# Two feed-forward openings reordered, one weight sum of each made by DMA, and 18 products ahead of the first load

## The chip, the core and the metric

The kernel runs on one core of a Trainium2 chip. Five engines work side by side, each on its own queue of instructions in a fixed order: TensorE (PE in the profile, with its weight loads as PEld), VectorE (DVE), ScalarE (ACT), GpSimd (POOL) and SyncE (SP). SP issues most DMAs, POOL a few of its own. An instruction starts when the one ahead of it on its queue has let it through and all that it waits for is done. The metric is the device time of one execution, in microseconds.

## The reference

One step of a decoder trunk on 520 tokens (512 of a prompt and 8 single samples), in float32:

```python
h = h + 0.5 * _swiglu(_rms_norm(h, ffn1_norm), w1_gate, w1_up, w1_down)
m, ... = _hybrid_mixer(_rms_norm(h, mix_norm), states, weights)   # pooling heads and a state-space scan
h = h + m
h = h + 0.5 * _swiglu(_rms_norm(h, ffn2_norm), w2_gate, w2_up, w2_down)
return _rms_norm(h, final_norm), new states

def _swiglu(x, wg, wu, wd):
    return (silu(x @ wg) * (x @ wu)) @ wd          # 1024 -> 2816 -> 1024
def _rms_norm(x, g):
    return x * rsqrt(mean(x * x) + 1e-6) * g
```

The change touches the first few microseconds of the two feed-forward parts, FFN1 and FFN2. Both compute the same thing from different weights.

## The kernel before

Activations stand transposed: 8 tiles of 128 features (D = 1024) by 520 tokens, the tokens in two halves of 260 (HB). A float32 product is made of three products in a faster format (`mm3`: L117, L120, L121): the weights are split into a high part `whi` (a cast on ACT, L107) and a low part `wlo` (a subtract on DVE, L108), the activations into `xth` and `xtl`.

Gate and up projection are a two-by-two block product over features and token halves, done by 7 products in place of 8 (class `Ffn`), as in Strassen's scheme. That needs sums of activations and sums of weights.

- For every block f of 128 columns of the 2816 (22 blocks) SP loads `raw` (two DMAs of 512 KB; `load`, L255 and L256). `raw` has two buffers. `whi`/`wlo` `a` is the split of its first half, `b` of a quarter of it. Weight sums: s1 is one DVE operation of 128x1024 (L262), s2 two of 128x512 (L263, L264), both split again into shi/slo `c` (of s1) and `d` (of s2).
- The seven products are numbered as in `product`; A (one PSUM bank) takes products 1, 6, 7 and 4, BE (two banks) takes 2, 5 and 3. A and BE have two buffers. After products 1, 6, 7 and 5 ACT copies the bank to `ac` (L299) before the next product goes on in it.
- The activations: `scaled` makes xg (x times the norm's gain, ACT, L181), `prep_pair` makes four differences xd of xg (DVE, L188 to L192) and splits xg and xd into `xth` (ACT, L195) and `xtl` (DVE, L196), for four pairs j = 0..3 of feature tiles.
- The norm's 1/rms isn't applied ahead of the products but behind them: `squares` sums the squares (ACT L157, DVE L158), `rstd` sums over partitions by a product with a tile of ones (psr, L163), takes the root on ACT (L164, which needs its own activation table; `ACT_TABLE_LOAD` in the trace) and the reciprocal on DVE (L165), for each token half. The result r_f is multiplied in behind the product.

**The openings.** While xg, its splits and r_f are being made, PE has nothing for the seven products. So the first blocks are done "plain": in float32 proper, without splits or sums (`plain`, L234; four P banks of each block; one such product leaves two records in the trace). FFN1 does f = 0 and f = 1 in this way (`direct` = 2), FFN2 only f = 0. `plain_out` finishes such a block: two multiplies by r_f on DVE (tg, L241), Silu on ACT (L243, again with a table load), two multiplies by the up half on DVE (L245), and the split of the result g (L247, L248). The first block by seven products is f = 2 in FFN1, and f = 1 in FFN2, whose weights are prepared under the mixer.

The order of the instructions of each engine isn't written out: a scheduler at build time places them by modelled times, with `tc.high_priority()` for parts that shall go early, and `tc.issue_after(ins)`, which lets nothing of the enclosed code that runs on the engine of `ins` be placed ahead of it. `behind[2]` holds the instruction behind which f = 2's load is placed: the second of `plain_out(0)`'s multiplies by r_f, in both FFNs. SP's loads wait for free buffers: f = 2's `raw` for the last product that reads f = 0's, f = 3's for the last readers of f = 2's first buffer, among them L264.

POOL does little here. It issues the loads of the states (br, hs) for the state output, which is worked into FFN2's stream.

Of the kernel before, what the change touches and what calls it, by code (L numbers as in the profile page):

```python
# [62 lines left out]
def tile_trunk_step(ctx: ExitStack, tc: tile.TileContext, ins: dict, outs: dict):  # L63
# [96 lines left out]
    def rstd(r, acc, hs, width, name):  # L160
        ps = bank(f"psr_{name}")[:, : hs.stop - hs.start]
        for k, sq in enumerate(acc):
            nc.tensor.matmul(ps, ones, sq, start=k == 0, stop=k == len(acc) - 1)  # L163
        nc.scalar.activation(out=r[:, hs], in_=ps, func=AF.Sqrt, bias=eps, scale=1.0 / width)  # L164
        nc.vector.reciprocal(out=r[:, hs], in_=r[:, hs])  # L165

    def rstds(nx, name):
        for b, hs in enumerate(HALVES):
            rstd(nx[3], [nx[2][:, hs]], hs, D, f"{name}{b}")
# [15 lines left out]
    def prep_pair(nx, gp, nb, xg, j, name):  # L185
        xth, xtl, _, _ = nx
        xd = gp.tile([P, 4, HB], F32, tag="g", bufs=nb, name=f"xd_{name}{j}")
        nc.vector.tensor_tensor(out=xd[:, 0:2], in0=xg[:, 0::2], in1=xg[:, 3:4].to_broadcast([P, 2, HB]),  # L188
                                op=ALU.subtract)
        nc.vector.scalar_tensor_tensor(out=xd[:, 2], in0=xd[:, 1], scalar=-1.0, in1=xg[:, 0], op0=ALU.mult,  # L190
                                       op1=ALU.subtract)
        nc.vector.scalar_tensor_tensor(out=xd[:, 3], in0=xd[:, 2], scalar=-1.0, in1=xg[:, 1], op0=ALU.mult,  # L192
                                       op1=ALU.subtract)
        for s, t in ((xg[:, 0:3], slice(0, 3)), (xd, slice(3, 7))):
            nc.scalar.copy(xth[:, j, t], s)  # L195
            nc.vector.tensor_tensor(out=xtl[:, j, t], in0=s, in1=xth[:, j, t].bitcast(F32), op=ALU.subtract)  # L196

    class Ffn:
# [52 lines left out]
        def load(self, f):  # L251
# [5 lines left out]
            d1 = split(raw[:, 0], 1024, f"{n}a", wp, 3, ("whi", "wlo"))  # L257
# [4 lines left out]
            nc.vector.tensor_tensor(out=s1, in0=diag, in1=up0, op=ALU.add)  # L262
# [14 lines left out]
        def product(self, f, p):  # L277
            js = range(KD // 2)
            if f not in self.A:
                with tc.issue_after(self.behind[f]) if f in self.behind else nullcontext():  # L280
                    self.load(f)
                n = f"{self.i}_{f}"
                self.A[f] = ps[0].tile([P, 512], F32, tag="A", bufs=2, name=f"A{n}")
                self.BE[f] = ps[0].tile([P, 2, 512], F32, tag="BE", bufs=2, name=f"BE{n}")
                self.ac[f] = [self.wx.tile([P, 2, HB], F32, tag="ac", bufs=3, name=f"ac{n}_{q}") for q in range(2)]
# [12 lines left out]
            if keep is not None:  # L298
                nc.scalar.copy(keep, out[:, :HB])  # L299
# [17 lines left out]
        def scales(self):  # L317
            rstds(self.nx, f"f{self.i}")
# [129 lines left out]
    xg1 = []  # L448
    for j in range(KD // 2):
# [9 lines left out]
        prep_pair(nx1, g1, NG, xg1[j], j, "f1")  # L459
    ffn1.plain_load(1)  # L460
    with tc.high_priority():
        ffn1.scales()
# [3 lines left out]
    with tc.high_priority():  # L466
        ffn1.behind[2] = ffn1.plain_out(0)
# [36 lines left out]
    def fill(j):  # L504
        if not j:
            f2["ffn"].plain_load(0)
        f2["ffn"].plain(0, f2[j], j)
        prep_pair(f2["ffn"].nx, f2["xg"], 4, f2[j], j, "f2")
# [613 lines left out]
```

## Time and profile before

| | |
|---|---|
| median of 3 runs | 993.05 us (991.81 to 993.05) |
| profiled execution | 992.8 us, span 991.0 us |
| granted TensorE clock (mean) | 0.997 |
| TensorE (PE) busy | 969.8 us, 98% |
| VectorE (DVE) busy | 800.0 us, 81% |
| ScalarE (ACT) busy | 552.8 us, 56% |
| GpSimd (POOL) busy | 87.4 us, 9% |
| HBM traffic | 114 GB/s over the span |
| FFN1's opening | from 0 to about 41 us |
| FFN2's opening | from about 637 to 655 us |

In a row of the timeline stand the start (us from the span's start), the duration, the engine, the line of the kernel, the operation, its output and inputs by the program's names, the shape and how many equal ones follow; in square brackets the idle time of that engine just before, and what ended it. A row of the waits names the waiting instruction, its releaser, and the total, the number and the longest of the waits in us. Busy times of PE are modelled ends of pipelined products, so a PE that is busy is not necessarily at its peak. The profiled execution's time is 1.8 us longer than its span.

### The profile page before, as it was taken

How to read it: one execution, taken by the hardware profiler on the slowest of the kernel's cores; microseconds unless marked ns; L12 is line 12 of the kernel's file. 1: busy time of each engine (PE TensorE's matmuls, PEld its weight loads, DVE VectorE, ACT ScalarE, POOL GpSimd, SP SyncE). 2: the span in 40 equal slices, each digit the busy share in tenths (PEclk: the TensorE clock that was granted, in tenths of full speed). 3: DMA queues.
4: the chain of work that ended last, by engine and by line, in shares of the span. 5: the costliest groups of instructions: out<-in, count | busy, mean ns of one | idle time of the engine just before them, and what ended most of it. 6: DMA issues, size and time to landing. Idle time of an engine off the chain costs nothing.

```text
span 991.0 us, 19414 instructions
## 1 busy us (share of the span) xinstructions
PE 969.8 (98%) x7852; PEld 951.0 (96%) x7852; DVE 800.0 (81%) x1295; ACT 552.8 (56%) x1011; POOL 87.4 (9%) x157
## 2 busy tenths in 40 slices
PE   7999999999999999999999999999999999999996
PEld 6899999999999999999899999899999999999995
DVE  7999656997569688788978997999967899668876
ACT  7566414664136455685668574666643566534653
POOL 0000000000000000156522000100013000120000
PEclk9999999999999999999999999999999999999998
DMA  6332322323222232262335232323246423363212
GB/s 188 121 128 95 120 86 86 128 86 129 85 86 81 91 126 85 82 206 100 124 114 186 81 125 86 113 98 128 100 117 198 162 88 127 120 181 119 96 65 87
DMA packets 42027, 114.48 MB, mean 116 GB/s; under 512 B 6408, under 2 KB 13512, under 8 KB 41936
## 3 DMA queue, kind: packets, MB, share of 16 engines
q1 hardware_dynamic: 38864, 103.78, 30.6%
q0 software_dynamic: 3072, 9.44, 3.7%
q8 instruction: 62, 1.02, 0.4%
q14 instruction: 29, 0.24, 0.1%
HBM read 105.86 MB, written 7.34 MB: 114 GB/s over the span
## 4 chain that ended last, share of the span: by engine, by line
PE 90%; DVE 5%; POOL 1%; DMA 1%; issue 1%; ACT 1%; SPq 0%; DVEq 0%; ACTq 0%
PE A L121 8%; PE A L117 8%; PE A L120 8%; PE dn L121 7%; PE dn L117 7%; PE dn L120 7%; PE BE L117 6%; PE BE L121 6%; PE BE L120 6%; PE wo L117 2%; PE wo L121 2%; PE wo L120 2%; PE P L234 2%; PE inz L117 2%; PE inz L121 2%; PE inz L120 2%
## 5 line engine op out<-in xcount | busy, mean ns | idle before, releaser
L117 PE MATMUL dn<-g,whi_1d 128*128 128x260 f32 x352 | 99.3, 283 | 0.2 <-DVE td L369 0.2
L120 PE MATMUL dn<-g,whi_1d 128*128 128x260 f32 x352 | 99.5, 283 | 0.0
L121 PE MATMUL dn<-g,wlo_1d 128*128 128x260 f32 x352 | 99.4, 283 | 0.0
L369 DVE SCALAR_TENSOR_TENSOR td<-dn,r_f 128x520 f32<-128x520 f32 x40 | 27.8, 698 | 72.7 <-PE dn L121 72.7
L121 PE MATMUL dn<-g,wlo_2d 128*128 128x260 f32 x256 | 72.5, 283 | 0.8 <-DVE wlo_2d L108 0.8
L117 PE MATMUL dn<-g,whi_2d 128*128 128x260 f32 x256 | 72.3, 282 | 0.0
L120 PE MATMUL dn<-g,whi_2d 128*128 128x260 f32 x256 | 72.3, 282 | 0.0
L117 PEld LDWEIGHTS dn<-g,whi_1d 128*128 128x128 f32 x352 | 66.1, 188 | 0.4 <-DVE td L369 0.4
L120 PEld LDWEIGHTS dn<-g,whi_1d 128*128 128x128 f32 x352 | 66.3, 188 | 0.0
L121 PEld LDWEIGHTS dn<-g,wlo_1d 128*128 128x128 f32 x352 | 66.2, 188 | 0.0
L299 ACT COPY ac<-A 128x260 f32<-128x260 f32 x123 | 45.6, 374 | 28.9 <-PE A L121 28.0
L107 ACT CAST whi_1d<-raw_1d 128x1024 fp32r<-128x1024 f32 (+1 forms) x24 | 23.5, 981 | 67.0 <-PE dn L120 54.2
L262 DVE TENSOR_TENSOR s<-raw 128x1024 f32<-128x1024 f32 x41 | 49.9, 1218 | 5.6 <-DMA raw<-in_w2gu 5.6
L234 PE MATMUL P<-xg_f,raw 128*128 128x260 f32 x192 | 45.4, 392 | 6.4 <-ACT sq_f L157 5.5
L121 PEld LDWEIGHTS dn<-g,wlo_2d 128*128 128x128 f32 x256 | 48.2, 188 | 1.0 <-DVE wlo_2d L108 1.0
L234 PEld LDWEIGHTS P<-xg_f,raw 128*128 128x128 f32 x192 | 36.9, 196 | 12.2 <-ACT sq_f L157 5.4
L117 PEld LDWEIGHTS dn<-g,whi_2d 128*128 128x128 f32 x256 | 48.3, 189 | 0.0
L120 PEld LDWEIGHTS dn<-g,whi_2d 128*128 128x128 f32 x256 | 48.2, 188 | 0.0
L117 PE MATMUL wo<-catg,whi_wo 128*128 128x260 f32 x128 | 37.2, 290 | 0.0
L117 PE MATMUL inz<-xh_mx,whi_inz 128*128 128x260 f32 x128 | 36.8, 287 | 0.1
L117 PE MATMUL inx<-xh_mx,whi_inx 128*128 128x260 f32 x128 | 36.4, 284 | 0.0
L121 PE MATMUL wo<-catg,wlo_wo 128*128 128x260 f32 x128 | 36.2, 283 | 0.0
(1341 smaller groups left out, 3936.7 us busy)
## 6 DMA issues: line engine op xcount, KB each, us to landing
raw<-in_w2gu SPq DMA_DIRECT2D x44, 512.0 KB, 4.5
raw<-in_w1gu SPq DMA_DIRECT2D x42, 512.0 KB, 4.5
raw_1d<-in_w1d SPq DMA_DIRECT2D x16, 512.0 KB, 4.5
raw_2d<-in_w2d SPq DMA_DIRECT2D x16, 512.0 KB, 4.4
raw_wo<-in_w_out SPq DMA_DIRECT2D x12, 512.0 KB, 4.9
ab<-scr_acs SPq DMA_DIRECT2D x8, 512.0 KB, 4.9
h<-in_state_ssm SPq DMA_DIRECT2D x16, 256.0 KB, 3.7
raw_inz<-in_w_in SPq DMA_DIRECT2D x8, 512.0 KB, 3.8
```

What stands on the lines that cost most here:

```text
L107: nc.scalar.copy(h, src)
L117: first = nc.tensor.matmul(ps, whi, xhi, start=start, stop=False, **kw)
L120: nc.tensor.matmul(ps, whi, xlo, start=False, stop=False, **kw)
L121: nc.tensor.matmul(ps, wlo, xhi, start=False, stop=stop, **kw)
L234: nc.tensor.matmul(self.banks[f, u][b][:, :HB], ws(self.raw[f][:, u], j + 4 * q), xg[:, slot[q]], start=j == q == 0, stop=j == 3 and q == ...
L262: nc.vector.tensor_tensor(out=s1, in0=diag, in1=up0, op=ALU.add)
L299: nc.scalar.copy(keep, out[:, :HB])
L369: nc.vector.scalar_tensor_tensor(out=t, in0=banks[d][:, :, :HB], scalar=-0.5, in1=self.nx[3].rearrange("p (b t) -> p b t", b=2), op0=ALU.mult,
```

## The change

1. 18 products of the 128x128 tile `ones` with itself are put at the head of PE's queue; nobody reads their bank.
2. FFN1: the split of the last pair's xd (j = 3; one ACT cast, one DVE subtract) is taken out of `prep_pair` and made later: the cast behind the second root on ACT, the subtract behind `plain_out(0)`'s second multiply by r_f (`free`) on DVE.
3. `mark`, a GpSimd copy of one column of the last xg, is placed on POOL. The DMAs of point 4 are placed behind it in FFN1.
4. For f = 2 of both FFNs s1 isn't summed on DVE. POOL issues three DMAs instead: two copy quarters of the weights from HBM into s1 (256 KB each), the third adds another quarter to both halves of s1 (512 KB, an accumulating DMA).
5. `behind` now has three parts: the split `a` is placed behind the first, the sums behind the second, and the third says whether s1 is made by DMA. FFN1: `(free,)`, then `(free, root, mark)`. FFN2: the last xd operation, then `plain_out(0)`'s `free`.
6. FFN2: product 1 of f = 1 is issued ahead of `scales`, and `scales` (psr, root, reciprocal) is placed behind that product's copy `ac` on ACT (`kept`) and behind the last `xtl` on DVE (`low`).

As the scheduler places it, only the two openings change their order: about the first 255 instructions of PE, and some 185 of them around FFN2's opening. SP's order stays as it is. On ACT, FFN1's shi_2c now stands ahead of whi_2a, whi_2b and Silu; in FFN2 shi_2c stands behind the cast of g. On PE, FFN2's product 1 of f = 2 now comes right behind product 1 of f = 1, and products 6, 7 and 4 of f = 1 follow each other.

```diff
@@ -88,6 +88,12 @@
     eps = cst.tile([P, 1], F32, tag="eps", name="eps")
     nc.vector.memset(eps, EPS)
 
+    def queued(*ins):
+        stack = ExitStack()
+        for i in ins:
+            stack.enter_context(tc.issue_after(i))
+        return stack
+
     def raw_pair(name):
         return wp.tile([P, 2, 1024], F32, tag="raw", bufs=2, name=f"raw_{name}")
 
@@ -161,12 +167,14 @@
         ps = bank(f"psr_{name}")[:, : hs.stop - hs.start]
         for k, sq in enumerate(acc):
             nc.tensor.matmul(ps, ones, sq, start=k == 0, stop=k == len(acc) - 1)
-        nc.scalar.activation(out=r[:, hs], in_=ps, func=AF.Sqrt, bias=eps, scale=1.0 / width)
+        root = nc.scalar.activation(out=r[:, hs], in_=ps, func=AF.Sqrt, bias=eps, scale=1.0 / width)
         nc.vector.reciprocal(out=r[:, hs], in_=r[:, hs])
+        return root.ins
 
     def rstds(nx, name):
         for b, hs in enumerate(HALVES):
-            rstd(nx[3], [nx[2][:, hs]], hs, D, f"{name}{b}")
+            root = rstd(nx[3], [nx[2][:, hs]], hs, D, f"{name}{b}")
+        return root
 
 
 
@@ -182,18 +190,25 @@
                                  scale=v(norm, d))
         return xg
 
-    def prep_pair(nx, gp, nb, xg, j, name):
+    def prep_pair(nx, gp, nb, xg, j, name, late=None):
         xth, xtl, _, _ = nx
         xd = gp.tile([P, 4, HB], F32, tag="g", bufs=nb, name=f"xd_{name}{j}")
         nc.vector.tensor_tensor(out=xd[:, 0:2], in0=xg[:, 0::2], in1=xg[:, 3:4].to_broadcast([P, 2, HB]),
                                 op=ALU.subtract)
         nc.vector.scalar_tensor_tensor(out=xd[:, 2], in0=xd[:, 1], scalar=-1.0, in1=xg[:, 0], op0=ALU.mult,
                                        op1=ALU.subtract)
-        nc.vector.scalar_tensor_tensor(out=xd[:, 3], in0=xd[:, 2], scalar=-1.0, in1=xg[:, 1], op0=ALU.mult,
-                                       op1=ALU.subtract)
-        for s, t in ((xg[:, 0:3], slice(0, 3)), (xd, slice(3, 7))):
+        last = nc.vector.scalar_tensor_tensor(out=xd[:, 3], in0=xd[:, 2], scalar=-1.0, in1=xg[:, 1], op0=ALU.mult,
+                                              op1=ALU.subtract)
+
+        def parts(s, t):
             nc.scalar.copy(xth[:, j, t], s)
-            nc.vector.tensor_tensor(out=xtl[:, j, t], in0=s, in1=xth[:, j, t].bitcast(F32), op=ALU.subtract)
+            return nc.vector.tensor_tensor(out=xtl[:, j, t], in0=s, in1=xth[:, j, t].bitcast(F32), op=ALU.subtract)
+
+        parts(xg[:, 0:3], slice(0, 3))
+        if late is not None:
+            late.append(lambda: parts(xd, slice(3, 7)))
+            return None
+        return last.ins, parts(xd, slice(3, 7)).ins
 
     class Ffn:
 
@@ -248,18 +263,30 @@
             nc.vector.tensor_tensor(out=g[:, 1], in0=tg, in1=g[:, 0].bitcast(F32), op=ALU.subtract)
             return free.ins
 
-        def load(self, f):
+        def load(self, f, first, then, by_dma):
             i, wx, src = self.i, self.wx, ins[f"w{self.i}gu"]
             n = f"{i}_{f}"
             raw = raw_pair(n)
             nc.sync.dma_start(out=raw[:, 0], in_=src[2 * f])
             nc.sync.dma_start(out=raw[:, 1], in_=src[2 * f + 1])
-            d1 = split(raw[:, 0], 1024, f"{n}a", wp, 3, ("whi", "wlo"))
+            with queued(*first):
+                d1 = split(raw[:, 0], 1024, f"{n}a", wp, 3, ("whi", "wlo"))
+            with queued(*then):
+                self.sums(f, n, src, raw, d1, by_dma)
+
+        def sums(self, f, n, src, raw, d1, by_dma):
+            wx = self.wx
             s1 = wx.tile([P, 2, 512], F32, tag="sw", bufs=2, name=f"s1_{n}")
             s2 = wx.tile([P, 2, 512], F32, tag="sw", bufs=2, name=f"s2_{n}")
             up0 = raw[:, 1, :512].unsqueeze(1).to_broadcast([P, 2, 512])
             diag = bass.AP(up0.tensor, up0.offset - 1024, [up0.ap[0], (1536, 2), up0.ap[2]])
-            nc.vector.tensor_tensor(out=s1, in0=diag, in1=up0, op=ALU.add)
+            if by_dma:
+                low = src[2 * f + 1][:, :512].unsqueeze(1).to_broadcast([P, 2, 512])
+                nc.gpsimd.dma_start(out=s1[:, 0], in_=src[2 * f][:, :512])
+                nc.gpsimd.dma_start(out=s1[:, 1], in_=src[2 * f + 1][:, 512:])
+                nc.gpsimd.dma_start(out=s1, in_=low, accum_op=ALU.add)
+            else:
+                nc.vector.tensor_tensor(out=s1, in0=diag, in1=up0, op=ALU.add)
             nc.vector.tensor_tensor(out=s2[:, 0], in0=s1[:, 1], in1=raw[:, 0, :512], op=ALU.add)
             nc.vector.tensor_tensor(out=s2[:, 1], in0=s2[:, 0], in1=raw[:, 0, 512:], op=ALU.add)
             e1 = split(s1.rearrange("p q c -> p (q c)"), 1024, f"{n}c", wx, 2, ("shi", "slo"))
@@ -277,8 +304,7 @@
         def product(self, f, p):
             js = range(KD // 2)
             if f not in self.A:
-                with tc.issue_after(self.behind[f]) if f in self.behind else nullcontext():
-                    self.load(f)
+                self.load(f, *self.behind.get(f, ((), (), False)))
                 n = f"{self.i}_{f}"
                 self.A[f] = ps[0].tile([P, 512], F32, tag="A", bufs=2, name=f"A{n}")
                 self.BE[f] = ps[0].tile([P, 2, 512], F32, tag="BE", bufs=2, name=f"BE{n}")
@@ -296,7 +322,7 @@
             a, c = self.ac[f]
             keep = {1: a[:, 0], 6: a[:, 1], 7: c[:, 0], 5: c[:, 1]}.get(p)
             if keep is not None:
-                nc.scalar.copy(keep, out[:, :HB])
+                self.kept = nc.scalar.copy(keep, out[:, :HB]).ins
             if p == 7:
                 nc.vector.tensor_tensor(out=c[:, 0], in0=c[:, 0], in1=c[:, 1], op=ALU.add)
 
@@ -315,7 +341,7 @@
             nc.vector.tensor_tensor(out=g[:, 1], in0=tg, in1=g[:, 0].bitcast(F32), op=ALU.subtract)
 
         def scales(self):
-            rstds(self.nx, f"f{self.i}")
+            return rstds(self.nx, f"f{self.i}")
 
         def rest(self, before, last_chunk):
             lo = 0
@@ -445,7 +471,10 @@
     ffn_psum("ppf1")
     nx1 = new_xt(xt1, "f1")
     ffn1 = Ffn(nx1, 1, wx1, g1, 2)
-    xg1 = []
+    xg1, late = [], []
+    warm = bank("warm")
+    for _ in range(18):
+        nc.tensor.matmul(warm[:, :P], ones, ones, start=True, stop=True)
     for j in range(KD // 2):
         for d in (j, j + KD // 2):
             q = slice(NVEC + d * NT if d else 0, NVEC + (d + 1) * NT)
@@ -456,15 +485,20 @@
             for d in (j, j + KD // 2):
                 squares(nx1, wx1, d, "f1")
         ffn1.plain(0, xg1[j], j)
-        prep_pair(nx1, g1, NG, xg1[j], j, "f1")
+        prep_pair(nx1, g1, NG, xg1[j], j, "f1", late if j == KD // 2 - 1 else None)
+    mark = tmp.tile([P, 1], F32, tag="mark", bufs=1, name="mark")
+    mark = nc.gpsimd.tensor_copy(mark, xg1[KD // 2 - 1][:, 1, :1]).ins
     ffn1.plain_load(1)
     with tc.high_priority():
-        ffn1.scales()
+        root = ffn1.scales()
     for u in range(2):
         for j in range(KD // 2):
             ffn1.plain(1, xg1[j], j, (u,))
     with tc.high_priority():
-        ffn1.behind[2] = ffn1.plain_out(0)
+        free = ffn1.plain_out(0)
+        with queued(root, free):
+            late.pop()()
+        ffn1.behind[2] = (free,), (free, root, mark), True
     ffn1.plain_out(1)
 
     nx2, xa = [], []
@@ -505,7 +539,7 @@
         if not j:
             f2["ffn"].plain_load(0)
         f2["ffn"].plain(0, f2[j], j)
-        prep_pair(f2["ffn"].nx, f2["xg"], 4, f2[j], j, "f2")
+        f2["last"], f2["low"] = prep_pair(f2["ffn"].nx, f2["xg"], 4, f2[j], j, "f2")
 
     ps[0] = tc.alloc_tile_pool(name="ppm", bufs=8, space=PSUM, reuse_waits="tile")
     mixer(tc, ins, outs, dict(locals()))
@@ -515,9 +549,11 @@
     f2["st"] = pool("st2", "left")
     f2["ffn"].states = f2["states"](f2["st"])
     next(f2["ffn"].states)
+    f2["ffn"].product(1, 1)
     with tc.high_priority():
-        f2["ffn"].scales()
-        f2["ffn"].behind[2] = f2["ffn"].plain_out(0)
+        with tc.issue_after(f2["ffn"].kept), tc.issue_after(f2["low"]):
+            f2["ffn"].scales()
+        f2["ffn"].behind[2] = (f2["last"],), (f2["ffn"].plain_out(0),), True
 
     last = act.tile([P, NT], F32, tag="acc", name="acc_last")
     res = []
```

## The prediction

> **What bounds the kernel now.** I read the page's busy table and chain first, then TensorE's waits, then both openings in the timeline.
>
> ```profile
> PE 969.8 (98%) x7852; PEld 951.0 (96%) x7852; DVE 800.0 (81%) x1295; ACT 552.8 (56%) x1011; POOL 87.4 (9%) x157
> PE 90%; DVE 5%; POOL 1%; DMA 1%; issue 1%; ACT 1%; SPq 0%; DVEq 0%; ACTq 0%
> ...
> PE P L234 <- ACT sq_f L157: 5.5, 1, 5.5
> PE A L117 <- ACT ac L299: 1.8, 2, 1.4
> PE P L234 <- DVE tg L241: 0.9, 1, 0.9
> ...
> PE BE L117 <- ACT ac L299: 0.2, 1, 0.2
> ```
>
> The first two are the page's busy row and its chain by engine: TensorE (PE) is the bound. The others are PE's waits (total, times, longest). The whole change acts on them: 5.5 us before the first product of FFN1's opening, 0.9 us inside that opening, 1.8 + 0.2 us in FFN2's. Nothing else in the program moves, so what the openings gain or lose stays until the end, where PE is 98% busy.
>
> FFN1's opening on PE (start us, duration, records; one fp32 product leaves two records), then stretches of it (length, PE busy and records, and so on; the column after POOL is the granted clock):
>
> ```profile
> 5.46 18.37 PE L234 MATMUL P<-xg_f,raw 128*128 128x260 f32 x76 [5.46 <-ACT sq_f L157]
> 23.67 1.04 PE L163 MATMUL psr_f<-acc_f,ones 128*128 128x260 f32 x4
> 24.55 4.55 PE L234 MATMUL P<-xg_f,raw 128*128 128x260 f32 x20
> 29.98 7.28 PE L234 MATMUL P<-xg_f,raw 128*128 128x260 f32 x32 [0.89 <-DVE tg L241]
> ...
> 5.46:8.30 2.84, 2.84 (x7) 2.26 (x8) 1.91 (x3) 1.86 (x3) 0.00 (x0) 1.00 1.04 330
> 8.30:10.00 1.70, 1.70 (x9) 1.50 (x8) 1.70 (x5) 1.70 (x4) 0.00 (x0) 1.00 0.96 304
> ```
>
> PE has work without a break from 5.46 to 29.1. Its first 7 records take 2.84/7 = 0.41 us each, the next 1.70/9 = 0.19. So the start is cold, though the granted clock reads 1.00, and costs 7 x 0.22 = 1.5 us.
>
> The two engines that feed it, ACT and then DVE:
>
> ```profile
> 16.92 0.73 ACT L181 ACTIVATE xg_f<-h 128x520 f32<-128x520 f32 x1
> 23.02 1.06 ACT L195 CAST xth_f<-xd_f 128x1040 fp32r<-128x1040 f32 x1 [3.15 <-DVE xd_f L192]
> 24.10 1.28 ACT L164 ACT_TABLE_LOAD   x1
> 25.39 0.85 ACT L164 ACTIVATE r_f<-psr_f,eps 128x260 f32<-128x260 f32 x2
> 26.50 1.04 ACT L107 CAST whi_2a<-raw 128x1024 fp32r<-128x1024 f32 x1 [0.26 <-DMA raw<-in_w1gu]
> 28.29 0.62 ACT L107 CAST whi_2b<-raw 128x512 fp32r<-128x512 f32 x1 [0.75 <-DMA raw<-in_w1gu]
> 40.16 1.05 ACT L107 CAST whi_3a<-raw 128x1024 fp32r<-128x1024 f32 x1 [1.03 <-DMA raw<-in_w1gu]
> ...
> 24.11 1.24 DVE L196 TENSOR_TENSOR xtl_f<-xd_f,xth_f 128x1040 fp32r<-128x1040 f32 x1 [1.12 <-ACT xth_f L195]
> 25.90 3.41 DVE L165 RECIPROCAL r_f<-r_f 128x260 f32<-128x260 f32 x2 [0.55 <-ACT r_f L164]
> 29.23 0.70 DVE L241 TENSOR_TENSOR tg<-P,r_f 128x260 f32<-128x260 f32 x2
> 29.85 1.22 DVE L108 TENSOR_TENSOR wlo_2a<-raw,whi_2a 128x1024 fp32r<-128x1024 f32 x1
> 30.98 1.22 DVE L262 TENSOR_TENSOR s<-raw 128x1024 f32<-128x1024 f32 x1
> 33.39 0.75 DVE L245 SCALAR_TENSOR_TENSOR tg<-P,tg 128x260 f32<-128x260 f32 x2
> 35.80 0.68 DVE L264 TENSOR_TENSOR s<-s,raw 128x512 f32<-128x512 f32 x1
> ```
>
> Read it as a chain. The last cast of xd (23.02) pushes the table load for Sqrt to 24.10, so the roots run at 25.39 although their sums (psr) were done at 24.7; then come the reciprocals, tg at 29.23, and PE's second half of the P products at 29.98.
>
> **The change part by part.**
>
> *The 18 products of ones.* They start once the 128x128 memset of ones is done, about 1.05 (it starts at 0.84 and takes 0.17), and leave 36 records of 128 columns. By columns (128/260) one record costs 0.20 us cold and 0.10 us warm. No row shows such records, so bounds: 36 x 0.10 = 3.6 us (end 4.7, fully under the present wait) and 36 x 0.20 = 7.2 us (end 8.3). I take the clock to rise 2.84 us after the first product, as above: 14 cold, 22 warm records, end near 6.1. The first P product then starts about 0.65 us later than 5.46, but warm: 1.5 - 0.65 = 0.85 us earlier at psr. Bounds at psr: 1.5 us earlier, or with all 36 cold 2.84 - 1.5 = 1.3 us later. The Trainium skill ("TensorE: Matmul & The Clock Gate", Part 1) says that the array runs at half clock until one window of about 3.4 us has been busy, and that the window runs freely; this trace's 2.84 us agrees within that freedom. By 3.4 us the warm-up would end near 6.4 instead, and the gain at psr would be 0.55 us.
>
> *The last xd cast and its low part moved behind Sqrt and tg.* The table load no longer follows the 23.02 cast but the one before it, and is done long before psr. The roots start with psr (near 23.3 instead of 25.39), the reciprocals' 3.41 us end near 27.1, and tg near 27.8. PE finishes its earlier records at 29.1 - 0.85 = 28.25 and goes straight on: the second half of P starts 1.7 us earlier. Bounds: 0.9 us later (warm-up all cold: 1.3 later less part of the wait of 0.89) and 2.4 earlier (0.89 + 1.5). The 1.06 cast and the 1.24 subtract still have to run, now at about 23.9 on ACT and 27.8 on DVE.
>
> *s1 by three software DMAs.* DVE loses one 1.22 us sum here. The three wait behind mark, which needs the last xg (16.92 + 0.73 = 17.65). The accumulating one waits for both copies, and POOL stands meanwhile. What the traces show of such transfers:
>
> ```profile
> 22.98 0.33 SPq L255 DMA_DIRECT2D raw<-in_w1gu  x1
> 36.55 0.33 SPq L255 DMA_DIRECT2D raw<-in_w1gu  x1
> ...
> hs<-in_state_ssm POOLq DMA_DIRECT2D x3, 256.0 KB, 4.3
> raw<-in_w2gu SPq DMA_DIRECT2D x2, 512.0 KB, 5.8
> ...
> raw<-in_w1gu SPq DMA_DIRECT2D x42, 512.0 KB, 4.5
> ```
>
> (The first two are SP's issues of f=2's and f=3's weights; then the landings between 634 and 646 us, where software and hardware queues met; then the page's median.) The copies go out at 17.9 and 18.4 and land by 22.7 (4.3 us). The accumulating 512 KB then meets f=2's weights, 1 MB that the faster P products release near 22.1 instead of 22.98. No row shows an accumulating DMA. From below: 4.5 us alone, L = 27.2. By plain bytes, f=2's weights land 0.87 us before the 28.29 at which their second half freed whi_2b, 27.4, and 512 KB more at 330 GB/s (the stretch at 5.46) add 1.6: L = 29.0. From above: it reads and writes its target, twice the bytes, so 27.4 + 3.2 = 30.6, and 1.3 more if the queues' meeting stretches it as it did 4.5 to 5.8: L = 31.9. I take 28.6, between the plain load and the byte count and nearer the latter, since the adding DMA's issue overlaps with the weights' transfer.
>
> What L does: ACT's new order has shi_2c (the cast of s1) ahead of whi_2a, whi_2b, Silu's table load and Silu. Behind it DVE runs wlo_2a, one s2 half, slo_2c, wlo_2b, two tg pairs and s2's second half (L264): 1.05 + 1.0 on ACT, then on DVE 1.13 for each full width (29.85 to 30.98), 0.6 to 0.68 for each half width and 0.7 for each pair: 2 x 1.13 + 2 x 0.6 + 2 x 0.7 + 0.68 = 5.55. So L264 ends at L + 7.6. It ended at 36.48. f=3's weights wait for it (issue 36.55, whi_3a at 40.16), and PE needs whi_3a next after f=2's first products. So the offset that leaves FFN1 is the later of -1.7 and L - 28.9: at 28.6 it is **-0.3 us**, from -1.7 (L = 27.2) to +3.0 (L = 31.9). DVE's free 1.22 us buys nothing: L is the cover that is gone. mark, a copy of one column, lies in POOL's idle time.
>
> *FFN2.* PE, ACT and DVE there:
>
> ```profile
> 640.04 0.39 PE L117 MATMUL A<-xth_f,shi_1d 128*128 128x260 f32 x1 [1.37 <-ACT ac L299]
> 642.32 0.39 PE L117 MATMUL A<-xth_f,shi_1c 128*128 128x260 f32 x1 [0.47 <-ACT ac L299]
> 643.88 0.28 PE L117 MATMUL BE<-xth_f,shi_1c 128*128 128x260 f32 x1
> ...
> 638.29 1.05 ACT L195 CAST xth_f<-xd_f 128x1040 fp32r<-128x1040 f32 x1
> 639.61 0.37 ACT L299 COPY ac<-A 128x260 f32<-128x260 f32 x1
> 642.29 1.28 ACT L243 ACT_TABLE_LOAD   x1
> 645.89 1.05 ACT L107 CAST shi_2c<-s 128x1024 fp32r<-128x1024 f32 x1
> ...
> 638.42 1.78 DVE L165 RECIPROCAL r_f<-r_f 128x260 f32<-128x260 f32 x1 [0.61 <-ACT r_f L164]
> 642.89 0.70 DVE L241 TENSOR_TENSOR tg<-P,r_f 128x260 f32<-128x260 f32 x2
> ```
>
> Now product (1,1)'s copy stands behind a cast and two roots, and PE waits 1.37. After: the roots wait for that copy and for the last xtl, and PE does f=2's first product in between, so the 1.37 goes. But products 6, 7 and 4 of f=1 now follow each other in one PSUM bank, where a product for another bank stood between the last two: two waits of 0.47. Both reciprocals now start after the last xtl: its cast ends at 639.34, 1.2 us of xtl, 3.41 of reciprocals, and tg begins at 643.9, 1 us later than 642.89. Behind it, in ACT's order, stand the table load (1.28, part of it beside tg), Silu 0.64, then DVE's pair 0.75, the g cast 0.63 and only then shi_2c 1.05: 644.6 + 0.8 + 0.64 + 0.75 + 0.63 + 1.05 = 648.5, instead of 646.9. PE gets there from 638.67 (the end of product (1,1): 640.04 - 1.37) by five products of 1.5 us (642.32 to 643.88) and 1.14 us of waits, at 647.3: a wait of 1.2. With 0.2 for f=2's wlo, a DVE operation now in the way, the sum is 0.2 + 0.94 + 1.2 = 2.3 against 1.37 + 0.47 + 0.2 = 2.04: **+0.3 us**, between -1.1 (the copies' 0.94 alone) and +1.2 (shi_2c another 0.9 late). The three DMAs are issued some 10 us before, and POOL's br and hs loads queue behind them; those feed the states computed beside these products, with a chunk in hand, so I cost them at nothing; uncovered they cost their landing, 4.3.
>
> *Sum.* Against the profiled execution's 992.8 (span 991.0 and 1.8 around it; the median of the runs is 993.05, 0.25 more): 992.8 - 0.3 + 0.3 = 992.8.
>
> **Rivals.**
> 1. *s1 lands early* (L at or below 27.3). Then FFN1 keeps 1.5 to 1.7, and FFN2 comes out between -1.0 and 0: 990.1 to 991.2, near 990.7. For it: 4.5 us for every 512 KB load. Against: 1 MB of weights in the same 5 us, and 5.8 us where queues met. The Trainium skill's rule for a software DMA ("DMA: Bandwidth & Descriptors", the anatomy of one DMA) is 2.0 us plus bytes over 436 GB/s, an estimate of 3.2 us for 512 KB, which would make this the case; hs's 4.3 us for half the bytes speaks against it.
> 2. *s1 lands late*, the other side: from L = 30.8 the blocked ACT queue holds f=3's weights back by over 1.9 us, and with FFN2's +0.3 the time passes 995.0. At L = 31.2, between 30.6 and 31.9: 992.8 + 2.3 + 0.3 = 995.4. For it: read and write of the target, and POOL's serial wait. Against: the plain byte count.
> 3. *The warm-up doesn't do what it says*: all 36 records cold, P's second half 0.9 later; f=3 then lies +0.9, and the time is 994.1. Against: the fall from 0.41 to 0.19.
>
> **How the numbers follow.** A measurement here tells about 0.2% (2.0 us) from no change. The forecast, openings that trade one wait for another: 0.48, with rival 3 at 0.06 of it. Rival 1 has 0.32, seven eighths of it under 991.05 (the median less 2.0); it rests on an L that no row shows. Rival 2 has 0.20, and 0.02 of the forecast's case lies above 995.05 with it. That gives faster 0.28, same 0.50, slower 0.22. The range goes from rival 1 with most of FFN2's gain, 990.0, to rival 2, 995.6; the likeliest case alone is 991.3 to 994.4.
>
> **What would show it.** After: P's records from about 6.1 on at 0.19 each; roots right behind psr, no wait of P for tg; shi_2c beginning at L, near 28.6, ACT waiting for a DMA just before it; whi_3a within 0.5 us of 40.16; in FFN2 no 1.37 wait, two near 0.47 on A, and one on shi_2c near 1.3. I am wrong if L is outside 27.5 to 30, if shi_2c in FFN2 comes before PE needs it, or if the added records end after 7.

## The result and the profile after

The changed kernel takes 1001.78 us (median of 4 runs, 1000.94 to 1003.62) against 992.46 us before: a ratio of 1.0096, with a 95% interval of 1.0084 to 1.0108. The forecast was 992.8 us, no change, with a range to 995.6; the kernel became 9.3 us slower, and the time lies outside the range.

The page of the changed kernel, its busy row and chain by engine, and then PE's waits:

```profile
PE 977.6 (98%) x7888; PEld 958.1 (96%) x7888; DVE 797.5 (80%) x1293; ACT 552.2 (55%) x1011; POOL 97.8 (10%) x164
PE 74%; issue 11%; DMA 5%; DVE 5%; ACT 2%; POOL 1%; SPq 1%; DVEq 0%; POOLq 0%; ACTq 0%
...
PE A L123 <- DVE tg L256: 6.0, 1, 6.0
PE pm L126 <- DVE catp L793: 1.7, 1, 1.7
PE BE L123 <- ACT shi_2c L113: 1.3, 1, 1.3
...
PE A L123 <- ACT ac L325: 0.9, 2, 0.5
```

Two waits are new and not in the forecast: 6.0 us in FFN1's opening, for a bank that DVE's tg frees, and 1.7 us for catp, which is in the mixer. The 0.9 us wait inside the P products is gone, and FFN2's are there as forecast.

FFN1's opening after: PE, then POOL, ACT, DVE and SP (timeline rows: start, duration, engine, line, operation; idle time before and its releaser in brackets).

```profile
1.06 6.15 PE L477 MATMUL warm<-ones 128*128 128x128 f32 x36 [1.06 <-DVE eps L89]
23.27 1.04 PE L169 MATMUL psr_f<-acc_f,ones 128*128 128x260 f32 x4
24.14 12.00 PE L249 MATMUL P<-xg_f,raw 128*128 128x260 f32 x54
42.19 0.56 PE L123 MATMUL A<-xth_f,whi_2a 128*128 128x260 f32 x1 [6.04 <-DVE tg L256]
...
17.70 4.97 POOL L490 COPY mark<-xg_f 128x1 f32<-128x1 f32 x1 [17.25 <-ACT xg_f L189]
22.61 0.70 POOL L285 DMA_DIRECT2D s<-in_w1gu  x1
23.30 0.55 POOL L286 DMA_DIRECT2D s<-in_w1gu  x1
29.94 1.25 POOL L287 DMA_DIRECT2D s<-in_w1gu  x1 [6.09 <-DVE xtl_f L205]
...
36.11 1.04 ACT L113 CAST shi_2c<-s 128x1024 fp32r<-128x1024 f32 x1 [10.35 <-DMA s<-in_w1gu]
37.06 1.04 ACT L113 CAST whi_2a<-raw 128x1024 fp32r<-128x1024 f32 x1
...
17.45 1.24 DVE L205 TENSOR_TENSOR xtl_f<-xd_f,xth_f 128x1040 fp32r<-128x1040 f32 x1
22.19 0.43 DVE L200 SCALAR_TENSOR_TENSOR xd_f<-xd_f,xg_f 128x260 f32<-128x260 f32 x1
24.42 3.42 DVE L171 RECIPROCAL r_f<-r_f 128x260 f32<-128x260 f32 x2 [1.79 <-ACT r_f L170]
42.96 0.69 DVE L291 TENSOR_TENSOR s<-s,raw 128x512 f32<-128x512 f32 x1
...
22.58 0.33 SPq L270 DMA_DIRECT2D raw<-in_w1gu  x1
43.72 0.33 SPq L270 DMA_DIRECT2D raw<-in_w1gu  x1
```

Read it from mark. The copy of one column (17.70) takes 4.97 us on POOL and ends at 22.67 (17.70 + 4.97), just when DVE's unbroken run ends (22.19 + 0.43 = 22.62). The two copies of s1 go out at 22.61 and 23.30, at the very moment at which SP issues f=2's weights (22.58). The adding DMA goes out at 29.94 and lands at 36.1. All of ACT's queue stands behind it: whi_2a, whose weights are there, starts at 37.06. L264 (now L291) runs at 42.96 instead of 35.80, and f=3's weights are issued at 43.72 instead of 36.55: +7.17 us.

The first P half is no loss: psr comes at 23.27 instead of 23.67, and the P products run through without the wait.

Where the span's 10.9 us went, by the start of the same product in the two traces: the mixer's first sum (psr_mx) at 370.72 and 378.01, FFN2's psr at 637.27 and 646.45, the last norm's sum (psl) at 967.2 and 977.8. So FFN1 carries +7.3, the mixer +1.9, FFN2 with what follows +1.4, and the tail +0.3. The mixer's order of instructions is the same in both kernels.

### The profile page after: what moved, and what is told of

Same layout as the page of the kernel before. It is cut to its first block, busy times and chain, and to the rows that moved or that the text cites. A ratio compares the mean times of both kernels' runs of the same rounds, so it can differ in the third digit from the quotient of the medians.

```text
span 1001.9 us, 19502 instructions
## 1 busy us (share of the span) xinstructions
PE 977.6 (98%) x7888; PEld 958.1 (96%) x7888; DVE 797.5 (80%) x1293; ACT 552.2 (55%) x1011; POOL 97.8 (10%) x164
## 4 chain that ended last, share of the span: by engine, by line
PE 74%; issue 11%; DMA 5%; DVE 5%; ACT 2%; POOL 1%; SPq 1%; DVEq 0%; POOLq 0%; ACTq 0%
PE A L127 6%; PE A L126 6%; PE A L123 6%; PE dn L127 6%; PE dn L123 6%; PE dn L126 6%; PE BE L127 5%; PE BE L123 5%; PE BE L126 5%; PE wo L123 2%; PE wo L127 2%; PE wo L126 2%; PE inz L123 2%; PE inz L126 2%; PE inz L127 2%
## 5 line engine op out<-in xcount | busy, mean ns | idle before, releaser
L325 ACT COPY ac<-A 128x260 f32<-128x260 f32 x123 | 45.6, 373 | 31.4 <-PE A L127 30.2
L289 DVE TENSOR_TENSOR s<-raw 128x1024 f32<-128x1024 f32 x39 | 47.6, 1220 | 6.0 <-DMA raw<-in_w2gu 6.0
L249 PEld LDWEIGHTS P<-xg_f,raw 128*128 128x128 f32 x192 | 35.9, 190 | 5.1
L123 PE MATMUL inx<-xh_mx,whi_inx 128*128 128x260 f32 x128 | 36.4, 285 | 0.0
```

What stands on the lines that cost most here:

```text
L123: first = nc.tensor.matmul(ps, whi, xhi, start=start, stop=False, **kw)
L249: nc.tensor.matmul(self.banks[f, u][b][:, :HB], ws(self.raw[f][:, u], j + 4 * q), xg[:, slot[q]], start=j == q == 0, stop=j == 3 and q == ...
L325: self.kept = nc.scalar.copy(keep, out[:, :HB]).ins
```

## The experiments

The letters in the expectations stand for these readings. A: GpSimd's mark could not read SBUF while VectorE's run lasted, and s1's late landing is FFN1's whole loss. B: the software DMAs themselves are held up while VectorE works. C: the late split or the warm-up costs by itself. D: FFN2 holds a real part of the loss. E: the mixer's part comes from an instruction fetch beside a small write. F: the mixer's part follows from FFN1's shift. G: part of the loss is the queue behind shi_2c on ACT.

The table gives, for every run, the median and its ratio to the kernel before with the interval, and from the profiled execution the offset of three milestones to those before (us): psr_mx (end of FFN1), FFN2's psr, and psl. One execution of each run was profiled, and it need not be a typical one: those of the change and of e6 are the longest of their four (1003.62 and 1003.81 us), that of e12 is the shortest of its ten (993.61).

| run | median us | ratio (95%) | psr_mx | psr_f | psl |
|---|---|---|---|---|---|
| the change | 1001.78 | 1.0096 (1.0084 to 1.0108) | +7.3 | +9.2 | +10.6 |
| e1_mark_memset | 1000.13 | 1.0064 (1.0041 to 1.0087) | +2.9 | +6.3 | +7.0 |
| e2_mark_dma | 1000.62 | 1.0076 (1.0059 to 1.0094) | +2.3 | +6.9 | +8.3 |
| e15_mark_recip | 1000.54 | one run | +2.7 | +6.2 | +7.7 |
| e8_shi_late | 1000.80 | 1.0079 (1.0062 to 1.0096) | +3.6 | +7.3 | +8.5 |
| e3_f1_dve | 996.56 | 1.0033 (1.0021 to 1.0045) | -0.2 | +3.7 | +4.4 |
| e6_no_warm | 1000.46 | 1.0085 (1.0064 to 1.0107) | +7.8 | +9.1 | +10.6 |
| e12_early_dma | 995.14 | 1.0024 (1.0015 to 1.0033) | -1.7 | +0.1 | +0.8 |
| e4_f2_only | 993.58 | 1.0008 (0.9998 to 1.0017) | 0.0 | +0.3 | +1.0 |
| e7_warm_only | 994.01 | 1.0015 (1.0005 to 1.0025) | -0.8 | +1.7 | +1.9 |
| e14_warm12_only | 992.69 | 0.9998 (0.9989 to 1.0007) | -0.7 | -0.3 | -0.1 |
| e10_late_only | 992.81 | 1.0003 (0.9994 to 1.0012) | +0.5 | -0.1 | -0.2 |
| e13_early_no_warm_f2_before | 993.15 | 1.0003 (0.9994 to 1.0012) | +0.6 | +0.3 | -0.3 |
| e16_parts | 992.19 | 0.9999 (0.9989 to 1.0010) | -1.2 | -1.3 | -0.7 |
| e17_parts_f2 | 992.94 | 1.0007 (0.9997 to 1.0017) | -1.1 | +0.2 | +1.3 |

### Mark without a read from SBUF, and without GpSimd's datapath

```diff
-    mark = nc.gpsimd.tensor_copy(mark, xg1[3][:, 1, :1]).ins
+    nc.scalar.copy(mk, xg1[3][:, 1, :1])          # e1
+    mark = nc.gpsimd.memset(mk, 0.0).ins
+    mark = nc.gpsimd.dma_start(out=mk, in_=xg1[3][:, 1, :1]).ins     # e2, instead
```

> The changed kernel, but mark is no longer a GpSimd copy that reads a column of xg: ACT copies the column, and GpSimd's mark is a memset over it, which reads nothing from SBUF. Theory A (GpSimd's copy took 4.97 us because it could not read SBUF while VectorE's run of operations from 17.45 to 22.62 lasted): the memset takes about 0.2 us near 17.9, the copies of s1 are issued near 18.2 and 18.7 and land near 22.5, the adding DMA is issued near 22.7 and lands near 29 to 30 (6.1 us, a little more beside f=2's weights), shi_2c starts there instead of at 36.11, and the kernel takes 994.5 to 996.5 us. Rival B (the software DMAs themselves are held up while VectorE works, and mark only stood in the same stretch): POOL's issue or the landing of the copies is as late as before, shi_2c stays later than 34, and the time stays above 999.

> The changed kernel, but mark is a small DMA of that column issued by POOL, so that GpSimd's own datapath is not used at all, only its DMA issue. Theory A: as with the memset, copies of s1 issued from about 18.3 on, shi_2c at 29 to 30.5, 994.5 to 996.5 us. Rival B: issue or landing of the copies held until VectorE's gap at 22.6, shi_2c later than 34, above 999 us.

POOL in the first and then the second of these runs, from their timelines, each with the landing of the adding DMA from its list of DMA issues:

```profile
18.63 0.10 POOL L491 MEMSET mark<- 128x1 f32 x1 [18.18 <-ACT mark L490]
18.67 0.69 POOL L285 DMA_DIRECT2D s<-in_w1gu  x1
23.21 1.24 POOL L287 DMA_DIRECT2D s<-in_w1gu  x1 [3.31 <-DMA s<-in_w1gu]
...
s<-in_w1gu POOLq DMA_DIRECT2D x1, 512.0 KB, 8.6
```

```profile
17.48 0.69 POOL L490 DMA_DIRECT2D mark<-xg_f  x1 [17.03 <-ACT xg_f L189]
18.16 0.55 POOL L285 DMA_DIRECT2D s<-in_w1gu  x1
22.51 1.24 POOL L287 DMA_DIRECT2D s<-in_w1gu  x1 [3.26 <-DMA s<-in_w1gu]
...
s<-in_w1gu POOLq DMA_DIRECT2D x1, 512.0 KB, 8.8
```

Mark is fast in both, the copies are issued between 18.2 and 19.4 and land in 3.1 us, in the midst of VectorE's run. So B falls, though the times, above 999, are those that it forecast; and A holds for mark. Two other runs that keep the GpSimd copy say the same: it takes 5.11 us in e8 and 5.32 in e6, and ends 0.05 us behind VectorE's run in both (22.41 and 22.36; 22.97 and 22.93). FFN1's loss goes from +7.3 to +2.9 and +2.3. But the times were forecast at 994.5 to 996.5 and came out at 1000: the adding DMA, now issued just beside f=2's weights, takes 8.6 to 8.8 us, so that s1 lands at 31.4 to 31.9, and the mixer adds 3.4 to 4.6 us in these runs (below).

### Mark during the reciprocals

```diff
+        with queued(root):
+            nc.scalar.copy(mk, xg1[3][:, 1, :1])
+            mark = nc.gpsimd.tensor_copy(mark, mk).ins
```

> The changed kernel, but mark is a GpSimd copy of a column that ACT writes right behind the second root, so that it starts near 25 while VectorE runs the two reciprocals (24.4 to 27.8, one input from SBUF each). Theory A in its narrow form (GpSimd's read waits only for VectorE operations with two inputs from SBUF): the copy takes 0.2 to 0.5 us. In its wide form (GpSimd waits for any gap of VectorE): the copy ends only at 27.8 or later, 2.8 us or more. The time of the kernel is not the question; with s1 this late it stays near 1000 us or more.

The run's timeline, POOL, DVE and ACT:

```profile
25.67 0.19 POOL L496 COPY mark<-mk 128x1 f32<-128x1 f32 x1 [25.22 <-ACT mk L494]
...
25.12 3.42 DVE L171 RECIPROCAL r_f<-r_f 128x260 f32<-128x260 f32 x2 [2.48 <-ACT r_f L170]
...
27.13 1.04 ACT L113 CAST whi_2a<-raw 128x1024 fp32r<-128x1024 f32 x1 [0.57 <-DMA raw<-in_w1gu]
36.44 1.05 ACT L113 CAST shi_2c<-s 128x1024 fp32r<-128x1024 f32 x1 [5.44 <-DMA s<-in_w1gu]
```

The same kind of copy takes 0.19 us in the midst of a busy VectorE, when VectorE's operation has one input from SBUF. It took 4.97 us beside a run of adds and subtracts with two. That is the narrow form, from one execution and one kind of one-input operation. The Trainium skill says so too ("GPSIMD Engine Reference", section 8, Key points): GpSimd shares its SBUF interfaces with VectorE and contends with operations that have two SBUF inputs. The two durations agree with it. The copies of s1, issued at 25.8 and 26.5, over 2 us behind f=2's weights (23.3), land in 3.3 us and the adding DMA in 5.9.

The edit did one thing more than was meant. With it the scheduler puts whi_2a, whi_2b and Silu's table load ahead of shi_2c on ACT. So s1 lands as late as in the changed kernel (36.44), but FFN1 loses only 2.7 us instead of 7.3. The next experiment makes this order on purpose.

### The queue behind shi_2c

```diff
-        ffn1.behind[2] = (free,), (free, root, mark), True
+        ffn1.behind[2] = (free,), (free, ffn1.silu, mark), True
```

> The changed kernel, mark as it is, but shi_2c placed behind plain_out(0)'s Silu on ACT, so that whi_2a, the table load and Silu no longer stand behind s1's landing at 36. Theory G (a part of the loss is the queue behind shi_2c on ACT, not the landing itself): whi_2a near 27.5, Silu near 30, only s2's first half on DVE waits for the landing, f=3's weights issued near 38 to 40 instead of 43.7: 996 to 999 us. Rival (the landing alone decides, whatever stands behind it): f=3's weights stay at 43 or later, 1001 us or more.

SP's row for f=3's weights in this run:

```profile
40.34 0.33 SPq L270 DMA_DIRECT2D raw<-in_w1gu  x1
```

Issued at 40.34 instead of 43.72, and FFN1's loss is 3.6 instead of 7.3 us with s1 as late as before (35.91): G holds, 3.7 us of FFN1's loss, and by e15 4.6, were the queue behind the landing and not the landing alone. The kernel's time was missed (1000.8 against 996 to 999 forecast), since the mixer took 3.7 us of its own.

### s1 back on VectorE, and s1 by an early DMA

```diff
-        ffn1.behind[2] = (free,), (free, root, mark), True
+        ffn1.behind[2] = (free,), (free, root), False                        # e3, mark left out
+            mark = nc.gpsimd.dma_start(out=mk, in_=xg1[2][:, 1, :1]).ins     # e12: mark from j = 2, s1 by DMA
```

> The changed kernel with FFN1's s1 summed on VectorE again and mark left out; the 18 products, the late split and FFN2's part stay. Theory A (FFN1's whole loss is s1's late landing): no 6.0 us wait of PE, whi_2a's first product near 35.5, f=3's weights issued near 35.5 to 36.5, FFN1 between -1.7 and 0 against the kernel before, FFN2 +0.3 to +1.0: 991.5 to 993.5 us. Rival C (the late split or the warm-up costs by itself): more than 2 us above the kernel before, 995 or more.

> The changed kernel, but mark is a small DMA of a column of the third pair's xg (written near 13.6) in place of a GpSimd copy of the last pair's. Theory A (s1's landing decides FFN1; with mark out of the way what is left is that copies and adding DMA meet f=2's weights, 31.4 to 31.9 in the two runs before): copies issued near 14.3 and 14.8 land near 19, the adding DMA lands near 25 to 26, ahead of or beside f=2's weights; shi_2c no longer last, f=3's weights issued between 35 and 36.6; FFN1 -1.5 to 0, mixer +2.5 to 3.5 (the 18 products are in it), FFN2 +0.8: 994 to 996.5 us. Rival (a software DMA lands late wherever it is put, or slows x and the weights of f=1): s1 later than 29 or P later by over 1 us, 997 us or more.

The early DMA run, POOL's adding DMA, ACT and SP:

```profile
19.71 1.24 POOL L287 DMA_DIRECT2D s<-in_w1gu  x1 [4.64 <-DMA s<-in_w1gu]
25.93 1.04 ACT L113 CAST shi_2c<-s 128x1024 fp32r<-128x1024 f32 x1 [0.59 <-DMA s<-in_w1gu]
34.65 0.33 SPq L270 DMA_DIRECT2D raw<-in_w1gu  x1
```

With s1 on VectorE FFN1 loses nothing (-0.2): A holds, and C falls for FFN1. With s1 landed at 25.9 FFN1 gains 1.7 us, the lower bound of the prediction's step (-1.7). How much of that is the landing's isn't shown: in this trace psr already stands 0.83 us earlier than before (22.84), and the 18 products alone (e7) leave FFN1 at -0.8. All landings with shi_2c ahead of whi_2a follow the prediction's rule, the later of -1.7 and L - 28.9: L = 25.9, FFN1 -1.7; 31.4, +2.3; 31.9, +2.9; 36.1, +7.3 (L - 28.9 gives 2.5, 3.0 and 7.2 for the last three). e8 and e15, where the casts of the weights go first, lie far below it: +3.6 at 35.9 and +2.7 at 36.4.

Yet s1 on VectorE ends 3.3 us above the kernel before by its ratio (0.0033 x 993), outside the forecast, and the early DMA 2.4. The traces put this to the mixer: +3.9 and +1.8.

### FFN2 alone

The 18 products, the late split, mark and FFN1's s1 by DMA are taken out: FFN1 is as before, FFN2 as changed.

> The kernel before with FFN2's part of the change alone (product 1 of f=1 ahead, the roots behind its copy, s1 by three DMAs). By the prediction's sum FFN2 is +0.3 us, by the changed kernel's waits (two of 0.45, one of 1.3, one of 0.3 against 2.04) +0.5 to +1.0: 992.8 to 993.5 us. Rival D (FFN2 holds a real part of the 9.3 us, as PE's offset to the kernel before grew from 9.5 to about 10.9 across it): 994 us or more.

The ratio gives +0.8 us (-0.2 to +1.7), the trace +1.0. Its waits are those of the changed kernel: 1.3 on shi_2c, two of 0.47, 0.3 on wlo_2a. D falls: it is about a tenth of the loss.

### The 18 products and the mixer

e6 is the changed kernel without the 18 products. e7 is the kernel before with the 18 products and nothing else, e14 the kernel before with 12 of them.

> The changed kernel without the 18 products. Theory E (the mixer's extra 2 to 3.5 us, which stands in the changed kernel and in all three runs with the 18 products but not in the run without them, comes from one 16 KB instruction fetch on a DMA ring, which the longer instruction stream of PE moves onto the 0.5 KB write scr_dt and makes land after 2.8 us instead of 1.3): the write lands in 1.3 us again, PE has no wait for catp, and the mixer adds nothing; mark is still late, so FFN1 stays at about +7: 999.5 to 1001 us. Rival F (the mixer's extra follows from the shift of everything by FFN1's loss, or from the other edits): the write stays at 2.8 us and catp's wait stays; 1001 to 1003 us.

> The kernel before with the 18 products alone. Theory E: FFN1 within 0.5 us of before (start of P 1.6 to 2.3 later, cold records gone), but the write scr_dt lands after 2.8 us and the mixer adds 2 to 3.5 us: 994.5 to 996.5 us. Rival F: no change beyond 1 us, 992 to 994 us.

> The kernel before with 12 products in place of 18 and nothing else. Theory E (it is where PE's next 16 KB of instructions are fetched, 0.12 us of products per record, that costs the mixer 2.4 us, and not the products as such): 12 records fewer are 12 x 0.12 = 1.4 us later for the fetch, past the 1.3 us in which scr_dt lands; scr_dt lands in 1.3 us, no wait of PE for catp, 991.8 to 993.2 us. Rival (any product ahead of the kernel costs the mixer so much): scr_dt still near 2.9 us and catp's wait near 1.5, 993.7 us or more.

The two runs that differ in the number of products alone, in the stretch from 409 to 412.2 us: the DMA engines' rate in 40 slices of 0.08 us, the instruction queue, the landing of scr_dt (dt, 0.5 KB, written to HBM and read back in another layout), and PE's wait in the mixer. First 18 products, then 12:

```profile
GB/s 0 0 0 0 0 0 0 0 0 205 0 4 2 0 0 0 0 0 0 0 0 0 0 0 0 0 0 0 0 0 0 0 0 0 0 0 0 0 0 0
q8 instruction: 1, 0.02, 2.3%
scr_dt<-dts SPq DMA_DIRECT2D x1, 0.5 KB, 2.9
...
PE pm L126 <- DVE catp L788: 1.5, 1, 1.5
```

```profile
GB/s 0 0 0 0 0 0 0 0 0 0 0 0 4 3 0 0 0 0 0 0 0 0 0 0 0 0 0 0 205 0 0 0 0 0 0 0 3 9 7 5
q8 instruction: 1, 0.02, 1.8%
scr_dt<-dts SPq DMA_DIRECT2D x1, 0.5 KB, 1.3
```

The 205 is one packet of 16 KB, the only one on the instruction queue in this stretch. With 18 products it passes at 409.8, right before the 0.5 KB of scr_dt (the 4 and 2), and the write's landing takes 2.9 us; with 12 it passes 1.5 us later (12 records of 0.12 us were forecast at 1.4), behind the write, which lands in 1.3. SP's read of scr_dt waits for that landing, DVE's work on it comes later, and PE waits 1.5 us for catp. The write's own bytes pass near 410.0 in both; only the landing is later, and why a packet that went ahead of them delays it, no trace shows. Without any products (e6) the write lands in 1.3 as well, and the wait for catp is gone.

All 16 traces agree: in the eight with 18 products the packet passes just ahead of the write's bytes, which land in 2.7 to 3.0 us, and PE waits 1.1 to 2.2 us for catp; in the eight with 12 or none, the kernel before among them, no such packet is ahead, the landing takes 1.3 us and catp's wait is 0.2 at most. E holds: the products as such cost nothing, 12 of them give 992.69 against 992.67. The median of e7, 994.01, lies between the two forecasts, so there the trace decides and not the time. F falls, with a rest: in e6 the mixer still added 1.3 us.

A part of that rest is the clock. The mixer of e3, and PE's granted clock in its third column from the right:

```profile
484.00:485.00 1.00, 0.74 (x4) 0.65 (x4) 1.00 (x3) 1.00 (x3) 1.00 (x2) 0.63 0.18 40
485.00:486.00 1.00, 1.00 (x6) 1.00 (x6) 1.00 (x2) 1.00 (x4) 1.00 (x1) 0.50 0.41 146
488.00:489.00 1.00, 1.00 (x11) 1.00 (x10) 1.00 (x3) 0.17 (x1) 0.12 (x1) 1.00 0.05 21
```

At half clock 6 products of 260 columns pass in a us instead of 11. Such a stretch of some 3.4 us behind PE's waits between 479 and 490 stands in the profiled executions of e1, e2, e3, e6, e8, e15 and e17, and in no other. Across it PE's offset to a run that has the same products and no such stretch grew by 1.2 us in e3 (against e7) and by 1.5 in e17 (against e16). It may come and go between executions of one kernel: of e3's ten runs the two shortest (993.59 and 994.26) have a mean granted clock of 0.998, the other eight (995.62 to 999.21) 0.995 or 0.996; but only one of the ten was profiled. What puts a run on one side or the other was not tried.

### The late split alone, and what is left when the costly parts go

Four runs build the change up again. e10 is the kernel before with the late split alone; e13 adds s1 of FFN1 by DMA behind the early mark; e16 adds 12 products to that; e17 adds FFN2 as changed.

> The kernel before with the late split of the last xd alone (no 18 products, s1 on VectorE, FFN2 as before). Prediction's step: the roots no longer stand behind the last cast and the table load, so tg comes about 1 us or more earlier and PE's wait of 0.9 us before the second half of P goes; VectorE then has the same operations left and f=3's weights, which wait for L264, decide. Expected -0.9 to +0.3 us: 991.5 to 993.3. Rival C (the late split costs by itself): 994 or more.

> What is left of the change when each part that cost something is taken out: no 18 products, FFN2 as before; the late split, and s1 of FFN1 by DMA with the early mark. Theory A: FFN1 -1.3 to -0.3, since VectorE is rid of 1.22 us ahead of L264, and nothing behind it changes: 991.2 to 992.7 against a kernel before at 992.7. Rival: the extra 1 MB ahead of f=1's weights and x holds P up, 993.5 us or more.

> The late split, s1 of FFN1 by DMA behind an early mark (a small DMA), 12 products instead of 18, FFN2 as before. If the parts add up: FFN1 -1.75 as with 18 products, scr_dt back at 1.3 us and no wait for catp as with 12 products alone, nothing else: -1.7 us, 990.5 to 991.5 beside a kernel before near 992.7. If they don't (the mixer or the tail takes the gain back): within 0.7 us of before.

> The same with FFN2's part of the change: 0.8 us more than the kernel without it (one wait of 1.3 on shi_2c, two of 0.47, one of 0.3, in place of 1.37 + 0.47 + 0.2): 991.2 to 992.5 us.

None of the four can be told from the kernel before; e10 came out within its forecast, e13 and e17 0.4 us above theirs. In e13 P's 76 records take 19.89 us instead of 18.37, and FFN1 loses 0.6. Its stretches, PE's records in the first bracket:

```profile
10.00:11.00 1.00, 1.00 (x3) 0.78 (x3) 0.77 (x2) 0.99 (x2) 0.00 (x0) 1.00 1.03 338
11.00:12.00 1.00, 1.00 (x5) 0.85 (x4) 1.00 (x3) 1.00 (x2) 0.00 (x0) 1.00 0.99 337
12.00:13.00 1.00, 1.00 (x7) 0.85 (x6) 1.00 (x2) 1.00 (x3) 0.00 (x0) 1.00 0.98 329
```

The slow pace of the start (3 to 5 records in a us) lasts from P's first record at 5.30 to past 11, and the early copies are issued only at 14.58. So P was not held up by the DMAs. e10, which has none of them, runs slow up to 10 and loses 0.5. One trace of each run can't tell what the early DMA is worth in FFN1, since the start alone moves psr by more than a us.

e16 was forecast 1.7 us below the kernel before. Its trace is 1.2 to 1.3 us ahead up to FFN2 and 0.7 at the end; its median is 992.19 against 992.32, and its interval, 0.1% either way, leaves the 1.7 out. So the parts don't add up to the forecast. e17 lies 0.75 us above e16, as forecast for FFN2, and within the noise. No version beats the kernel before by what can be measured.

## Why the prediction was wrong

- **What bounds it.** Right: the openings' waits decide, PE is 98% busy. "Nothing else in the program moves" was wrong. The order in the mixer didn't move, but the point at which a packet of instructions is fetched did, and it met a 0.5 KB write some 400 us later. The mixer added 1.9 us here, 1.7 of it PE's wait for catp.
- **The products.** 6.15 us against 5.0 forecast from 14 cold and 22 warm records. Stretches of the changed kernel, PE's records in the first bracket:

```profile
3.00:4.00 1.00, 1.00 (x7) 1.00 (x6) 0.00 (x0) 0.30 (x1) 0.00 (x0) 1.00 0.92 338
4.00:5.00 1.00, 1.00 (x6) 1.00 (x6) 0.00 (x0) 1.00 (x3) 0.00 (x0) 1.00 1.06 264
5.00:6.00 1.00, 1.00 (x11) 1.00 (x10) 0.48 (x1) 1.00 (x2) 0.00 (x0) 1.00 0.96 336
```

  The pace doubled near 5.0 here, 4 us after the first product instead of 2.84, and over 1 us later in e3 (7 records between 5 and 6). psr gained 0.4 us of the 0.85 forecast. One trace's 2.84 us was taken for a constant; over all traces the slow start lasts from 2.84 us (before) to about 6 (e13, from 5.30 to past 11). The Trainium skill's freely running window ("TensorE: Matmul & The Clock Gate", Part 1) fits such a spread better than one figure; the page gives 0.5 us either way for it, and the traces here show more.
- **The late split.** Right: PE's 0.9 us wait went, and P ended 1.1 us earlier (24.14 + 12.00 against 29.98 + 7.28; 1.7 forecast, and 0.45 of the difference is what the products didn't give).
- **s1 by DMA: the step that failed.** "mark, a copy of one column, lies in POOL's idle time" costed mark by its size. It took 4.97 us, because DVE was in a run of two-input operations. That moved the copies from 17.9 to 22.6, onto f=2's weights, where they took 5.6 and 6.1 us instead of 4.3; then the adding DMA took 6.1. L became 36.1, above the upper end of 31.9. That is 7.5 us above the 28.6 of the sum, and mark made 4.2 to 4.7 of them: with a fast mark L was 31.4 and 31.9. The other 2.8 to 3.3 us are a second term that was too small, the adding DMA beside f=2's weights: it took 8.6 to 8.8 us when it was issued within a us of them. Issued at least 2.4 us ahead of them or 7 us behind, it took 5.8 to 6.3, near a plain load's 4.5 and 1.6 more for the doubled bytes; the prediction kept the doubling for its upper end.
- **What L does.** Right to 0.1 us: L264 at L + 7.6 says 43.7, the end was 43.65, and the offset L - 28.9 = 7.2 was 7.17 for f=3's weights. The mechanism of rival 2 happened, at a landing that its price didn't reach.
- **A cost that was not seen.** PE stood still for 6.0 us, and its clock fell, as stretches of 1 us show (products in the first bracket, granted clock third from the right):

```profile
38.00:39.00 1.00, 0.00 (x0) 0.00 (x0) 0.86 (x1) 0.98 (x3) 0.00 (x0) 1.00 0.00 0
39.00:40.00 1.00, 0.00 (x0) 0.00 (x0) 1.00 (x3) 0.99 (x2) 0.00 (x0) 0.57 0.00 0
43.00:44.00 1.00, 1.00 (x6) 1.00 (x6) 0.85 (x3) 0.97 (x3) 0.00 (x0) 0.50 0.00 0
46.00:47.00 1.00, 1.00 (x10) 1.00 (x10) 0.91 (x2) 0.16 (x1) 0.00 (x0) 1.00 0.95 377
```

  The first products of f=2 ran at half speed: the offset went from +5.3 at whi_2a (42.19) to +7.0 at whi_3a (48.49). It cost nothing on top: PE began with whi_3a 0.05 us behind the end of its cast (47.39 + 1.05), so at full speed it would have waited for f=3's weights.
- **FFN2.** Right in its parts: 0.3, two of 0.47 and 1.3 us were measured for 0.2, two of 0.47 and 1.2. The sum was +0.3; these waits make +0.5, and the run with FFN2 alone gives +0.8 (-0.2 to +1.7). PE has no wait that br or hs would explain, as forecast.
- **Rivals.** Rival 2, a late landing, is what happened, at an offset of 7.2 us instead of its 2.3, and most of it for a reason that it didn't give (mark). Rival 1 (early landing) needed other edits: e12 has FFN1 at -1.7 with L = 25.9, part of it by the start. Rival 3 didn't happen: P ran warm.

## What to carry to other kernels

An instruction that only marks a moment costs what its engine must wait for, not what it moves: ask what the other engines do at that moment and whether that can hold it up. Before a transfer replaces an operation, see what its landing stands ahead of on the queue that consumes it: here one cast in front of ready work was half of FFN1's loss or more. And a difference far from an edit, in code whose order didn't move, is to be looked up in the DMA queues and the clock before it is put down to the edit.

## What the runs showed of the hardware

- GpSimd's copy of one column of 128 partitions took 0.19 us beside VectorE's reciprocals (one SBUF input; e15) and 4.97 to 5.32 us beside a run of its two-input operations (the change, e8, e6), until that run ended; beside the same run of operations a GpSimd memset took 0.10 us (e1) and a DMA issue 0.69 (e2).
- An accumulating DMA of 512 KB into SBUF landed in 5.8 to 6.3 us when it was issued over 2 us ahead of 1 MB of plain loads or well behind them, and in 8.6 to 8.8 us when issued within a us of them (e1, e2); the median of a plain load of 512 KB is 4.5.
- With a 16 KB instruction fetch on the DMA engines right ahead of a 0.5 KB write, the write's landing took 2.7 to 3.0 us instead of 1.3 (eight traces against eight). Six products more or less at the head of PE's queue decided whether the two met, 400 us later.
- The granted clock fell to 0.50 in a 6 us idle of PE in the changed kernel, some 3 us after the last product, and rose again some 3 us after the next (1.00 at 46). It also fell behind a stretch of shorter waits in the mixer, in seven of 16 traces, for about 3.4 us.
- The first records of PE ran at half pace for 2.84 us (before) to about 6 us (e13), while the granted clock in the profile's rows read 1.00.
